# Strided attention on one core: another order of the first loads, TensorE's loop without its empty rounds, one tile for the blocks

## The chip, the core and the metric

The kernel runs on one core of a Trainium2 chip. The metric is the device time of one execution in microseconds, as a median over runs. The engines' names are those of the profile: PE is TensorE (PEld its weight loads), DVE VectorE, ACT ScalarE, POOL GpSimd, SP SyncE. SP computes nothing here; it issues every DMA, in the order of its program, and the sixteen DMA engines move the bytes. One DMA is one load or one store below.

## The reference

Every query attends to the 16 positions 0, 64, 128, ... of its own batch and head (8 x 12 heads, 1,024 positions, 64 values each).

```python
attend_positions = np.arange(0, seq, stride)
k = K[:, :, attend_positions, :].copy()
v = V[:, :, attend_positions, :].copy()
scores = np.einsum('bhqd,bhkd->bhqk', q, k) * scale
weights = np.exp(scores - np.max(scores, axis=-1, keepdims=True))
weights = weights / (np.sum(weights, axis=-1, keepdims=True) + 1e-10)
result[:, :, i, :] = np.einsum('bhqk,bhkd->bhqd', weights, v)[:, :, 0, :]
```

Q is 25.2 MB and so is the output, all float32. Of K and V only the 1,536 rows of 256 bytes at the attended positions are read, 384 KB each.

## The kernel before

The 96 heads are cut into 24 groups of four. A group's queries are one block of 1 MB, which lies in one of 18 buffers of 128 x 2,048 float32 (`qn`). A group's output is written into the buffer that held its queries, and stored from there. The buffers are nine tiles of two neighbours each (`pairs`), so that one store can send two groups, 2 MB. Loads are cut into 32 rows of 32 KB (`load`, issued through the helper at line 34).

For each group g the steps are:

- `cast`: the block is rounded to bfloat16 (`qb`) on POOL. For groups 0, 1 and 2 ACT takes one half (line 299) and POOL the other (line 301).
- `transpose` on DVE (line 316) into `qt`.
- `scores`: 16 matmuls on TensorE (line 324) with the prepared keys `k_t`.
- `largest` on DVE (lines 338 and 341), `raise_` on ACT (the exponential, line 346), `sums` on DVE (lines 351 and 354), `weights` on POOL (line 358).
- `turn`: four transposes of the weights on TensorE (line 365), then `spread` on ACT (line 377).
- `outputs`: eight matmuls (line 385) with the prepared values `v_all`, and `evict` on ACT (line 403), which brings the result from PSUM into the group's buffer.
- `queue`: the store on SP, and behind it late loads.

The keys are rounded once on ACT (line 263), transposed on DVE (line 264) and copied into `k_t` by DVE and ACT (line 273). The values are copied into `v_all` (line 287): the first eight small copies on POOL between its casts 0 and 1, the others later on ACT and POOL.

`Program` records every step with what it reads and writes and then gives each engine its instructions in the order in which they were recorded, with the semaphore waits between engines. `ORDER` (line 491) sets that order for the steady part. SP's order is: keys, Q block 0, values, Q blocks 1 to 17, and then what `queue` records. Since a late load takes the place of a stored group, it waits until that store has landed, and SP issues nothing else meanwhile.

TensorE's instructions are a loop of 13 turns of two rounds (`pe_stream`). Round i makes the scores of group i, the turn of group i - 2 and the outputs of group i - 3. Three counters, the gates `turned`, `weighted` and `free`, let a step begin. The last two rounds have no group of their own: their scores are made of old data and nobody reads them, and two memsets of one column of `edge` on DVE (line 314) open the gate for them. The outputs of group 23 stand behind the loop.

The last store, of group 23, is issued by itself at the end of the program, behind the wait of SP for the last eviction, while POOL waits for all older stores to land.

Of the kernel before, what the change touches and what calls it, by code (L numbers as in the profile page):

```python
# [10 lines left out]
FP32 = mybir.dt.float32  # L11
# [7 lines left out]
def _ap_with(ap: bass.AP, new_ap, extra_offset: int = 0) -> bass.AP:  # L19
    return dataclasses.replace(  # L20
        ap, ap=[list(p) for p in new_ap], offset=ap.offset + extra_offset
    )


def _copy(nc, out: bass.AP, in_: bass.AP):

    sides = [
        mybir.BassSymbolicTensorAccessPattern(
            ap=side.ap, dtype=side.dtype, bass_ap=side,
            is_dma=True, for_custom_bir_dma=True,  # L30
        )
        for side in (in_, out)
    ]
    return nc.sync.add_instruction(  # L34
        mybir.InstDMACopy(
            name=nc.get_next_instruction_name(), engine=mybir.EngineType.SP,
            ins=sides[:1], outs=sides[1:], queue="qSPDynamicHW",
            mode="Copy",
        )
    )  # L40


class Program:
# [13 lines left out]
    def op(self, engine, fn, reads=(), writes=(), after=(), lane=None, gate=None, gates=(), times=1, looped=False, last=False):  # L57
        i = len(self.ops)
        deps, own = set(after), set()
        for k in reads:  # L60
            deps.add(self.writer.get(k))
            own.add(self.writer.get(k))
        for k in writes:
            deps.update(self.readers.get(k, ()))
            deps.add(self.writer.get(k))
            own.add(self.writer.get(k))
        deps.discard(None)
        for k in reads:
            self.readers.setdefault(k, []).append(i)
        for k in writes:  # L70
            self.writer[k], self.readers[k] = i, []
        self.ops.append(dict(
            engine=engine, fn=fn, lane=lane or engine, deps=deps, own=own,
            gate=gate, gates=gates, times=times, last=last, looped=looped,
        ))
        return i
# [92 lines left out]
def kernel(  # L169
# [8 lines left out]
    nc = tc.nc  # L178

    B, H, S, D = Q.shape  # L180
# [3 lines left out]
    P = 128  # L184
    HG = 4
    NG = B * H // HG
    NC = NG // 2
    SD = S * D
    TURN = 2
    assert B * H == NG * HG and S == 1024 and D == 64 and NK == 16 and NG % TURN == 0  # L190
    BUFS = 18
    RUN = 2
    assert NG % RUN == 0 and BUFS % RUN == 0

    sb = ctx.enter_context(tc.tile_pool(name="sb", bufs=1))
    ps = ctx.enter_context(tc.tile_pool(name="ps", bufs=1, space=bass.MemoryType.PSUM))

    edge = sb.tile([P, 32], FP32, name="edge")
    pairs = [sb.tile([P, RUN, 32 * D], FP32, name=f"pair{i}") for i in range(BUFS // RUN)]
    qn = [pairs[i // RUN][:, i % RUN] for i in range(BUFS)]  # L200
    k_raw = sb.tile([P, NC, D], FP32, name="k_raw")
    k_bf, k_r = [sb.tile([P, NC, D], BF16, name=f"k_half{i}") for i in range(2)]
    v_raw = sb.tile([P, NC, D], FP32, name="v_raw")
# [20 lines left out]
    op = prog.op  # L224

    def load(g):
        n = 32
        op("SP", lambda: _copy(
            nc, qn[g % BUFS],
            _ap_with(Q, [[HG * SD // n, n], [1, HG * SD // n]], g * HG * SD),  # L230
        ), writes=[f"qn{g % BUFS}{h}" for h in range(2)], lane=f"q{g % BUFS}")
# [3 lines left out]
    def load_rows(name, tile_, src, lane):  # L235
        op("SP", lambda: nc.sync.dma_start(tile_, _ap_with(src, kv_src)),
           writes=[name], lane=lane)

    load_rows("k_raw", k_raw, K, "k")
    load(0)  # L240
    load_rows("v_raw", v_raw, V, "v")
    for g in range(1, BUFS):
        load(g)

    op("POOL", lambda: nc.gpsimd.memset(identity, 0.0), writes=["identity"])
# [1 line left out]
        out=identity, in_=identity, compare_op=ALU.not_equal, fill=1.0, base=0,  # L247
# [8 lines left out]
        out=sel, in_=identity.rearrange("p (q h k) -> p h q k", h=2, k=NK),  # L256
        op=ALU.max, axis=mybir.AxisListType.XY,
# [52 lines left out]
    def transpose(g):  # L310
        k_in = {0: "0", 1: "1"}.get(g)
        words = qt[g % 2].bitcast(I32)
        if g >= NG:
            op("DVE", lambda: nc.vector.memset(edge[:, g - NG : g - NG + 1], 0.0), gate="turned")
            return
        op("DVE", lambda: nc.vector.transpose(  # L316
            _ap_with(words, [words.ap[0], [1, 2], [D, 16], [2, 32]]), qb[g % 2].bitcast(I32),
        ), reads=[f"qb{g % 2}0", f"qb{g % 2}1"] + [f"k_t{k_in}{h}" for h in range(4) if k_in],
           writes=[f"qt{g % 2}"], gate="turned")
# [11 lines left out]
    def scores(g):  # L331
        op("PE", None, reads=[f"qt{g % 2}"] + [f"k_t{g % 2}{h}" for h in range(4)],
           writes=[f"sc{g % 2}"], gates=[("turned", g + 1)], looped=True)
# [23 lines left out]
    def weights(g):  # L357
        op("POOL", lambda: nc.gpsimd.tensor_tensor(  # L358
            out=wt[g % 2], in0=ex[g % 2],
            in1=rec[g % 2].unsqueeze(2).to_broadcast([P, 32, NK]), op=ALU.mult,  # L360
        ), reads=[f"ex{g % 2}", f"rec{g % 2}"] + [k for k in apart if k[0] == "v"], writes=[f"wt{g % 2}"], gate="weighted")

    def turn_products(g):
        for c in range(4):
            r = nc.tensor.transpose(  # L365
                tp_ps[g % 2][:, 2 * c : 2 * c + 2].rearrange("p a b -> p (a b)"),
                wt[g % 2][:, 8 * c : 8 * c + 8].rearrange("p t k -> p (t k)"), identity,
            )
        return r
# [12 lines left out]
    def output_products(g, k):  # L382
        for c in range(4):
            for u in range(2):
                r = nc.tensor.matmul(  # L385
                    _ap_with(
                        o_ps, [o_ps.ap[0], [128, 2], [256, 2], [1, D]],
                        extra_offset=512 * c + D * u,
                    ),
                    lhsT=wb[g % 2][:, 2 * c + u],  # L390
                    rhs=v_all[:, k].rearrange("p s d -> p (s d)"), start=True, stop=True,
                )
        return r
# [14 lines left out]
    def send(g, n):  # L408
        return _copy(
            nc,  # L410
            _ap_with(out, [[16 * D, P], [2 * SD, 2 * n], [1, 16 * D]], g * HG * SD),
            _ap_with(qn[g % BUFS], [pairs[0].ap[0], [1, 1], [1, 32 * n * D]]),
        )

    def store(g, n):
        op("SP", lambda: send(g, n), lane=f"out{g % BUFS // n}of{n}",
           reads=[f"qn{i % BUFS}{h}" for i in range(g, g + n) for h in range(2)])

    def idle(i):
# [29 lines left out]
    VALUES = {0: [(*q, "ACT") for q in large[:2]], 1: [(*q, "ACT") for q in large[2:4]]}  # L449
    VALUES.update((i + 2, [large[4 + i]]) for i in range(4))  # L450

    turns = (NG + 2) // TURN

    def queue(g):
        if g == NG - 2:
            store(g, 1)
        elif g % RUN == RUN - 1 and g < NG - 1:
            store(g - RUN + 1, RUN)
            late = BUFS + g - 2 * RUN + 1
            if BUFS <= late < NG:  # L460
                for n in range(late, late + RUN):
                    load(n)

    def at(i, stage, lag):
        g = i - lag
        if g in early.get(stage, ()):
            return
        if stage == "transpose" and 0 <= g < NG + 2:
            transpose(g)
        elif stage == "scores" and 0 <= g < NG + 2:  # L470
            scores(g)
        elif stage == "weights" and 0 <= g < NG:
            weights(g)
        elif stage == "turn" and 0 <= g < NG:
            turn(g)
        elif stage == "out" and -1 <= g < NG:
            outputs(g)
        elif stage == "spread" and 0 <= g < NG:
            spread(g)
        elif stage == "evict" and 0 <= g < NG:  # L480
            evict(g)
        elif stage == "cast" and 0 <= g < NG:
            cast(g, False)
        elif stage == "values" and g in VALUES:
            for q in VALUES[g]:
                values(*q)
        elif 0 <= g < NG and stage in stages:
            stages[stage](g)
# [3 lines left out]
    for i in range(1, NG + 5):  # L492
        for step in ORDER:
            name = step.rstrip("-0123456789")
            at(i, name, int(step[len(name):]))

    def pe_stream(sems, gates):
        pe = nc.tensor
        done = sems["PE"]
        pe.sem_inc(gates["weighted"], 2)  # L500
        pe.sem_inc(gates["free"], 3)
        with pe.Fori(0, turns) as turn_:
            for j in range(TURN):
                i = turn_ * TURN + j
                pe.wait_ge(gates["turned"], j + 1)
                score_products(j, i).then_inc(done, 1)
                pe.wait_ge(gates["weighted"], j + 1)
                turn_products(j).then_inc(done, 1)
                pe.wait_ge(gates["free"], j + 1)
                output_products(j + 1, i).then_inc(done, 1)  # L510
            for name in ("turned", "weighted", "free"):
                pe.sem_inc(gates[name], -TURN)

    pending, sems = prog.emit(pe_stream)
    with tc.tile_critical(sync_engine=mybir.EngineType.Pool, no_gpsimd_drain=True) as landed:
# [39 lines left out]
```

## Time and profile before

| | |
|---|---|
| median of 3 runs | 128.17 us (127.93 to 128.45) |
| the profiled execution, its own time | 127.63 us |
| its span, first to last instruction | 125.8 us |
| HBM read and written | 25.95 MB and 25.17 MB |
| mean rate over the span | 406 GB/s |
| loads of Q blocks | 24 of 1 MB |
| stores | 11 of 2 MB, 2 of 1 MB |
| granted clock of TensorE, mean | 0.867 |

How to read the lines of the profile that follow: a row of the timeline has start, duration, engine, line, operation and the tiles that it writes and reads (`pair<-in_Q_dram` is a load of a Q block, `out_dram<-pair` a store; buffer numbers are left out), a count, and in brackets the idle time before it with what ended it. SPq is SP's queue of instructions; its duration is that of the issue, not of the transfer. A row of DMA issues has a count, the size of one and the median time from issue to landing. A row of windows has the stretch, its length, busy time with the number of instructions of PE, PEld, DVE, ACT and POOL, the granted clock, the mean busy share of the DMA engines and GB/s; a packet's bytes are counted where the packet starts, so short stretches can show more or less than the true flow.

### The profile page before, as it was taken

The page shows a single profiled execution, that of the slowest core. Times are in us where ns is not written, and L with a number is a line of the kernel's source. Part 1 is how long each engine was busy: PE and PEld are TensorE (multiplying, and loading weights), DVE is VectorE, ACT ScalarE, POOL GpSimd, SP SyncE. Part 2 cuts the span into 40 slices and gives each one's busy share as a digit, 9 for nine tenths or more (in the row PEclk, how much of TensorE's full clock was granted, in tenths as well). Part 3 has the DMA queues.
Part 4 walks back from the last instruction along what each step waited for, and adds up shares of the span by engine and source line. Part 5 has one row for each costly group of instructions (what it writes and reads, how often), then busy time and mean ns, then how long its engine had stood idle before and what let it go on. Part 6 is the DMA issues. An engine that isn't in the chain of part 4 may idle for free.

```text
span 125.8 us, 2084 instructions
## 1 busy us (share of the span) xinstructions
PE 58.1 (46%) x736; PEld 43.5 (35%) x736; DVE 87.1 (69%) x131; ACT 93.8 (75%) x109; POOL 75.9 (60%) x67
## 2 busy tenths in 40 slices
PE   0007672556489466665555565666656533000000
PEld 0006452445366444443443344444434321000000
DVE  3795879999979899999999999999966100000000
ACT  4266756999888999999999999999999965000000
POOL 5648589999998688889888888879233300000000
PEclk9999999998555999999999999999999975555555
DMA  1998989989899998999999999999999999999991
GB/s 41 425 406 385 490 365 479 448 385 479 365 479 437 406 469 354 422 422 479 417 391 458 422 385 432 464 406 424 417 422 422 427 427 437 427 432 417 406 424 65
DMA packets 6132, 51.15 MB, mean 406 GB/s; under 512 B 3696, under 2 KB 3696, under 8 KB 3696
## 3 DMA queue, kind: packets, MB, share of 16 engines
q1 hardware_dynamic: 6128, 51.12, 96.8%
q14 instruction: 4, 0.03, 0.1%
HBM read 25.95 MB, written 25.17 MB: 406 GB/s over the span
## 4 chain that ended last, share of the span: by engine, by line
ACT 51%; POOL 15%; DVE 7%; DMA 5%; PE 4%; issue 1%; SPq 1%; POOLq 0%
ACT pair L403 28%; ACT wb_all L377 16%; ACT ex L346 7%; POOL qb L305 6%; DMA v_raw<-in_V_dram 5%; POOL wt_all L358 4%; PE o L385 4%; POOL v_all L287 4%; DVE qt L316 3%; DVE total L351 1%; DVE top L338 1%; DVE rec L354 1%; POOL qb L301 1%; SPq L34 1%; DVE low L341 1%
## 5 line engine op out<-in xcount | busy, mean ns | idle before, releaser
L403 ACT COPY pair<-o 128x2048 f32<-128x2048 f32 x24 | 47.9, 1995 | 2.8 <-PE o L385 2.8
L305 POOL CAST qb<-pair 128x2048 bf16<-128x2048 f32 x21 | 39.7, 1892 | 1.5 <-DMA pair<-in_Q_dram 1.5
L385 PE MATMUL o<-v_all,wb_all 128*128 (+1 forms) x216 | 31.6, 295 | 8.2 <-ACT pair L403 8.2
L358 POOL TENSOR_TENSOR wt_all<-ex,rec 128x512 bf16<-128x512 f32 x24 | 25.4, 1058 | 15.4 <-DVE rec L354 15.1
L377 ACT ACTIVATE wb_all<-tp,sel 128x512 bf16<-128x512 bf16 x48 | 33.3, 810 | 0.7 <-PE tp L365 0.6
L316 DVE STREAM_TRANSPOSE qt<-qb 128x1024 int32<-128x1024 int32 x24 | 29.8, 1242 | 1.2 <-POOL qb L305 0.7
L385 PEld LDWEIGHTS o<-v_all,wb_all 128*128 128x128 bf16 x216 | 20.7, 105 | 14.9 <-issue 9.6
L324 PE MATMUL sc<-k_t,qt 128*128 x416 | 19.4, 200 | 12.9 <-DVE qt L316 12.8
L324 PEld LDWEIGHTS sc<-k_t,qt 128*128 128x128 bf16 x416 | 16.9, 103 | 17.5 <-issue 16.6
L365 PE MATMUL tp<-identity,wt_all 128*128 128x128 bf16 x104 | 11.1, 235 | 25.5 <-POOL wt_all L358 25.5
L346 ACT ACTIVATE ex<-low 128x512 f32<-128x512 f32 x24 | 18.3, 764 | 2.5 <-DVE low L341 2.5
L351 DVE TENSOR_REDUCE total<-ex 128x32 f32<-128x512 f32 x24 | 16.3, 678 | 3.9 <-ACT ex L346 3.9
L341 DVE TENSOR_TENSOR low<-sc,top 128x512 f32<-128x512 f32 x24 | 16.6, 691 | 0.8
L365 PEld LDWEIGHTS tp<-identity,wt_all 128*128 128x128 bf16 x104 | 6.4, 103 | 28.3 <-POOL wt_all L358 28.2
L338 DVE TENSOR_REDUCE top<-sc 128x32 f32<-128x512 f32 x24 | 15.2, 632 | 1.3 <-PE sc L324 1.3
L354 DVE RECIPROCAL rec<-total 128x32 f32<-128x32 f32 x24 | 8.5, 353 | 0.8
L287 POOL CAST v_all<-v_raw 32x128 bf16<-32x128 f32 (+1 forms) x12 | 5.2, 431 | 1.5 <-DMA v_raw<-in_V_dram 0.8
L299 ACT CAST qb<-pair 128x1024 bf16<-128x1024 f32 x3 | 3.1, 1045 | 3.1 <-DMA pair<-in_Q_dram 3.1
L301 POOL CAST qb<-pair 128x1024 bf16<-128x1024 f32 x3 | 3.1, 1039 | 3.3 <-DMA pair<-in_Q_dram 3.3
L259 POOL MEMSET v_all<- 128x3456 f32 x1 | 3.0, 2979 | 0.0
L287 ACT CAST v_all<-v_raw 32x640 bf16<-32x640 f32 x4 | 2.9, 722 | 0.0
L250 DVE MEMSET k_t<- 128x1664 uint32 x1 | 1.4, 1445 | 1.9 <-issue 1.9
(15 smaller groups left out, 9.6 us busy)
## 6 DMA issues: line engine op xcount, KB each, us to landing
pair<-in_Q_dram SPq DMA_DIRECT2D x24, 1024.0 KB, 15.0
out_dram<-pair SPq DMA_DIRECT2D x11, 2048.0 KB, 22.8
out_dram<-pair SPq DMA_DIRECT2D x2, 1024.0 KB, 18.7
k_raw<-in_K_dram SPq DMA_DIRECT2D x1, 384.0 KB, 3.9
v_raw<-in_V_dram SPq DMA_DIRECT2D x1, 384.0 KB, 6.8
```

What stands on the lines that cost most here:

```text
L305: op("POOL", lambda: nc.gpsimd.tensor_copy(out=b, in_=q), reads=[f"qn{g % BUFS}{h}" for h in range(2)] + apart, writes=[f"qb{g % 2}{h}" fo ...
L316: op("DVE", lambda: nc.vector.transpose(_ap_with(words, [words.ap[0], [1, 2], [D, 16], [2, 32]]), qb[g % 2].bitcast(I32),), reads=[f"qb{g ...
L324: r = nc.tensor.matmul(sc_ps[g % 2][:, 64 * i : 64 * i + 64], lhsT=_ap_with(qt[g % 2], [qt[g % 2].ap[0], [2, P]], extra_offset=2 * P * i + f),
L338: op("DVE", lambda: nc.vector.tensor_reduce(out=m, in_=s, op=ALU.max, axis=mybir.AxisListType.X,), reads=[f"sc{g % 2}"], writes=[f"top{g % ...
L341: op("DVE", lambda: nc.vector.tensor_tensor(out=low, in0=s, in1=m.unsqueeze(2).to_broadcast([P, 32, NK]), op=ALU.subtract,), reads=[f"sc{g ...
L346: op("ACT", lambda: nc.scalar.activation(out=ex[g % 2], in_=low, func=AF.Exp, bias=0.0, scale=scale,), reads=["low"], writes=[f"ex{g % 2}"])
L351: op("DVE", lambda: nc.vector.tensor_reduce(out=total[g % 2], in_=ex[g % 2], op=ALU.add, axis=mybir.AxisListType.X,), reads=[f"ex{g % 2}"] ...
L358: op("POOL", lambda: nc.gpsimd.tensor_tensor(out=wt[g % 2], in0=ex[g % 2], in1=rec[g % 2].unsqueeze(2).to_broadcast([P, 32, NK]), op=ALU.mult,
L365: r = nc.tensor.transpose(tp_ps[g % 2][:, 2 * c : 2 * c + 2].rearrange("p a b -> p (a b)"), wt[g % 2][:, 8 * c : 8 * c + 8].rearrange("p t ...
L377: op("ACT", lambda a=a: nc.scalar.activation(out=wb[g % 2][:, :, 64 * a : 64 * a + 64], in_=tp_ps[g % 2], func=AF.Copy, scale=sel[:, a : a ...
L385: r = nc.tensor.matmul(_ap_with(o_ps, [o_ps.ap[0], [128, 2], [256, 2], [1, D]], extra_offset=512 * c + D * u,), lhsT=wb[g % 2][:, 2 * c + ...
L403: op("ACT", lambda: nc.scalar.copy(to, o_ps.rearrange("p c (b x) -> p c b x", b=2)), reads=["o"], writes=[f"qn{g % BUFS}{n}" for n in rang ...
```

## The change

It has three parts. The first loads go out as Q block 0, keys, Q block 1, values, Q blocks 2 to 17. TensorE's loop has 12 turns, so it covers the 24 groups alone; the turns of groups 22 and 23 and the outputs of groups 21 and 22 follow it as straight code, and the two rounds of empty scores and their memsets are gone. The 18 buffers are one tile, `q_all`; the runs of groups that one store sends are written as a table (11 of two groups, then group 22 alone), and the late loads are taken from a list.

```diff
-    RUN = 2
+    RUNS = {**{g: 2 for g in range(0, NG - 2, 2)}, NG - 2: 1}
+    ENDS = {g + n - 1: (g, n) for g, n in RUNS.items()}
...
-    pairs = [sb.tile([P, RUN, 32 * D], FP32, name=f"pair{i}") for i in range(BUFS // RUN)]
-    qn = [pairs[i // RUN][:, i % RUN] for i in range(BUFS)]
+    q_all = sb.tile([P, BUFS, 32 * D], FP32, name="q_all")
+    qn = [q_all[:, i] for i in range(BUFS)]
...
+    load(0)
     load_rows("k_raw", k_raw, K, "k")
-    load(0)
+    load(1)
     load_rows("v_raw", v_raw, V, "v")
-    for g in range(1, BUFS):
+    for g in range(2, BUFS):
         load(g)
...
-        if g >= NG:
-            op("DVE", lambda: nc.vector.memset(edge[:, g - NG : g - NG + 1], 0.0), gate="turned")
-            return
...
-        op("SP", lambda: send(g, n), lane=f"out{g % BUFS // n}of{n}",
+        op("SP", lambda: send(g, n), lane=f"out{g % BUFS}",
...
-    turns = (NG + 2) // TURN
+    turns = NG // TURN
+
+    late = list(range(BUFS, NG))
 
     def queue(g):
-        if g == NG - 2:
-            store(g, 1)
-        elif g % RUN == RUN - 1 and g < NG - 1:
-            store(g - RUN + 1, RUN)
-            late = BUFS + g - 2 * RUN + 1
-            if BUFS <= late < NG:
-                for n in range(late, late + RUN):
-                    load(n)
+        if g not in ENDS:
+            return
+        first, n = ENDS[g]
+        store(first, n)
+        while late and late[0] - BUFS < first:
+            load(late.pop(0))
...
+        for j in range(2):
+            pe.wait_ge(gates["weighted"], j + 1)
+            turn_products(j).then_inc(done, 1)
+            pe.wait_ge(gates["free"], j + 1)
+            output_products(j + 1, NG + j).then_inc(done, 1)
```

More of the change, by code (lines that the diff above doesn't have):

```diff
@@ L191 @@
     BUFS = 18
-    RUN = 2
-    assert NG % RUN == 0 and BUFS % RUN == 0
+    RUNS = {**{g: 2 for g in range(0, NG - 2, 2)}, NG - 2: 1}
+    ENDS = {g + n - 1: (g, n) for g, n in RUNS.items()}
     sb = ctx.enter_context(tc.tile_pool(name="sb", bufs=1))
@@ L411, in send @@
             _ap_with(out, [[16 * D, P], [2 * SD, 2 * n], [1, 16 * D]], g * HG * SD),
-            _ap_with(qn[g % BUFS], [pairs[0].ap[0], [1, 1], [1, 32 * n * D]]),
+            _ap_with(qn[g % BUFS], [q_all.ap[0], [1, 1], [1, 32 * n * D]]),
         )
     def store(g, n):
-        op("SP", lambda: send(g, n), lane=f"out{g % BUFS // n}of{n}",
+        op("SP", lambda: send(g, n), lane=f"out{g % BUFS}",
            reads=[f"qn{i % BUFS}{h}" for i in range(g, g + n) for h in range(2)])
@@ L467, in at @@
             return
-        if stage == "transpose" and 0 <= g < NG + 2:
+        if stage == "transpose" and 0 <= g < NG:
             transpose(g)
-        elif stage == "scores" and 0 <= g < NG + 2:
+        elif stage == "scores" and 0 <= g < NG:
             scores(g)
```

## The prediction

> **What bounds the kernel now.** I read the page's slices and DMA parts first, because the table of engines shows none above 75%.
>
> ```profile
> span 125.8 us, 2084 instructions
> PE 58.1 (46%) x736; PEld 43.5 (35%) x736; DVE 87.1 (69%) x131; ACT 93.8 (75%) x109; POOL 75.9 (60%) x67
> DMA  1998989989899998999999999999999999999991
> q1 hardware_dynamic: 6128, 51.12, 96.8%
> ACT 51%; POOL 15%; DVE 7%; DMA 5%; PE 4%; issue 1%; SPq 1%; POOLq 0%
> ```
>
> The sixteen DMA engines are busy in every slice but the first and the last, for 96.8% of the span, all on the one queue that SP feeds. The chain that ended last names ACT, but it is followed back from the last engine instruction, so what happens after that instruction isn't in it. The timeline of the end shows the difference, and the issues from 106 us on show how long the last store took.
>
> ```profile
> 102.88 0.54 SPq L34 DMA_DIRECT2D out_dram<-pair  x1
> 104.83 1.87 ACT L403 COPY pair<-o 128x2048 f32<-128x2048 f32 x1 [1.98 <-PE o L385]
> 107.28 0.54 SPq L34 DMA_DIRECT2D out_dram<-pair  x1
> out_dram<-pair SPq DMA_DIRECT2D x1, 1024.0 KB, 19.7
> out_dram<-pair SPq DMA_DIRECT2D x1, 1024.0 KB, 17.8
> ```
>
> The last eviction ends at 106.70. The last store is issued at 107.28 and lands 17.8 later, at 125.1; the one before it goes out at 102.88 and lands 19.7 later, at 122.6. All arithmetic is over 18 us before the end, and those 18 us are stores that wait for their turn.
>
> That transfers wait in line all along shows in the rates by stretch (last column GB/s) and in the times to landing.
>
> ```profile
> 15.00:40.00 25.00, 15.97 (x202) 12.61 (x197) 22.56 (x34) 21.11 (x27) 23.14 (x19) 0.82 1.02 438
> 40.00:70.00 30.00, 18.21 (x247) 13.56 (x245) 29.01 (x43) 30.00 (x36) 25.07 (x18) 0.98 0.99 422
> 70.00:100.00 30.00, 17.25 (x244) 12.82 (x241) 25.19 (x42) 30.00 (x35) 18.71 (x14) 1.00 1.00 424
> 100.00:122.00 22.00, 2.83 (x16) 1.61 (x15) 0.00 (x0) 4.67 (x4) 0.00 (x0) 0.56 1.00 425
> out_dram<-pair SPq DMA_DIRECT2D x11, 2048.0 KB, 22.8
> ```
>
> The rate is 422 to 438 whatever the engines do. A 2 MB store moves in 2.097 MB / 424 = 4.9 us, yet it lands 22.8 us after its issue: some 18 us of other transfers lie ahead of it. So the span is one line of transfers, and its end is start of the line + what the line loses before it runs at full rate + bytes / rate. Only the first two can change here.
>
> **The start of the line.** These are SP's first issues and the first work that each load releases, then the rates in the first microseconds.
>
> ```profile
> 0.96 0.43 SPq L236 DMA_DIRECT2D k_raw<-in_K_dram  x1
> 1.45 0.74 SPq L34 DMA_DIRECT2D pair<-in_Q_dram  x1
> 3.10 12.33 SPq L34 DMA_DIRECT2D pair<-in_Q_dram  x17
> 4.86 0.83 ACT L263 CAST k_half<-k_raw 128x768 bf16<-128x768 f32 x1 [2.26 <-DMA k_raw<-in_K_dram]
> 7.29 1.04 ACT L299 CAST qb<-pair 128x1024 bf16<-128x1024 f32 x1 [1.60 <-DMA pair<-in_Q_dram]
> 9.13 2.75 POOL L287 CAST v_all<-v_raw 32x128 bf16<-32x128 f32 x8 [0.77 <-DMA v_raw<-in_V_dram]
> 11.47 1.04 ACT L299 CAST qb<-pair 128x1024 bf16<-128x1024 f32 x1 [1.04 <-DMA pair<-in_Q_dram]
> 13.87 1.05 ACT L299 CAST qb<-pair 128x1024 bf16<-128x1024 f32 x1 [0.50 <-DMA pair<-in_Q_dram]
> 1.50:2.00 0.50, 0.00 (x0) 0.00 (x0) 0.10 (x1) 0.50 (x1) 0.26 (x2) 1.00 0.07 16
> 2.00:3.00 1.00, 0.00 (x0) 0.00 (x0) 1.00 (x1) 0.60 (x1) 1.00 (x2) 1.00 0.39 86
> 3.00:4.00 1.00, 0.00 (x0) 0.00 (x0) 0.83 (x2) 0.00 (x0) 1.00 (x1) 1.00 1.21 261
> ```
>
> The releases are 4.86 (keys), 7.29 (Q block 0), 9.13 (values), 11.47 (Q block 1), 13.87 (Q block 2). So inside the line a Q block costs 2.34 to 2.43 us (I use 2.40), and the values, of the same size and shape as the keys, cost 9.13 - 7.29 = 1.84. The keys, first in the line, cost 4.86 - 0.96 = 3.90 from their issue: 2.06 more than the values. The rates say where a part of this lies: from 2 to 3 us only 86 GB/s flow, then 261, which is the rate of these 256-byte rows. What moved in that microsecond would take 86 / 261 = 0.33, so **0.67 us is lost in a slow first microsecond**. The other 2.06 - 0.67 = 1.39 is issue, first byte and landing, which any first transfer pays.
>
> **The change, part by part.**
>
> *Order of the first loads.* The same four transfers, with Q block 0 moved ahead of the keys and Q block 1 ahead of the values, on the same queue; two DMA issues pass two others on SP, nothing is added. The sum of the four inside the line is unchanged (2 x 2.40 + 2 x 1.84 = 8.48). What changes is who pays the slow first microsecond. No row shows a Q block at the head of an empty line, so I bound it. If the slowness belongs to the keys (1,536 small rows, and few of them under way at first), a Q block of large rows skips it and the keys' own slow beginning passes while Q block 0 moves for 2.4 us: gain 0.67. If it belongs to the first microsecond of any transfer, the gain is 0. The issue of a Q block is also longer than that of the keys, 0.74 against 0.43 in the rows above: loss up to 0.31. But that 0.74 was taken behind another issue. Later, behind a wait, two of them took 1.11 (row below), so one takes some 0.55, and I take 0.10. Of the ramp's two bounds I take 0.67, because what is short in that microsecond looks like rows: 86 GB/s are 336 rows of 256 bytes in 1 us, and 261 are 1,020, while the code cuts a whole Q block into 32 pieces. A limit on rows that lets 336 through doesn't touch 32. **Gain 0.67 - 0.10 = 0.57; bounds -0.31 and +0.67.**
>
> ```profile
> 60.72 1.11 SPq L34 DMA_DIRECT2D pair<-in_Q_dram  x2
> ```
>
> *What is late because of it.* With the gain, Q block 0 lands at 0.96 + 1.49 + 2.40 = 4.85, the keys at 6.69, Q block 1 at 9.09, the values at 10.93. On ACT the rounding of the keys waits in front of its half of cast 0, so cast 0 now follows the keys; on DVE the key copies and transpose 0 follow them. The keys are 1.83 later and the values 1.80, so all arithmetic starts about 1.8 us later. Its cover: the last eviction then ends at 108.5 and the last store enters the line near 109.1, while the line is full up to the landing of the store before it, then 122.6 - 0.57 = 122.0. That leaves over 12 us. The first store is the other place: it is issued at 29.60, and the last of the first 18 loads, whose issue of some 0.6 ends at 3.10 + 12.33 = 15.43, lands at 14.8 + 35.5 = 50.3, so 1.8 us later still finds 18 us of line. Cost 0; without that cover it would be 1.8.
>
> ```profile
> 29.60 8.83 SPq L34 DMA_DIRECT2D out_dram<-pair  x2
> pair<-in_Q_dram SPq DMA_DIRECT2D x1, 1024.0 KB, 35.5
> 55.39 1.30 SPq L34 DMA_DIRECT2D pair<-in_Q_dram  x2
> SPq L34 <- DMA out_dram<-pair: 28.2, 3, 17.0
> ```
>
> *Late loads.* Load 18 waits on SP for the first store to land, at 55.39, and everything behind it on SP waits too. Before, the store of groups g-1 and g is followed by loads g+15 and g+16 (18 and 19 behind groups 2 and 3). After, it is followed by the loads n with n - 18 below g-1: again 18 and 19 there, then 20, 21 and 22, 23. Same order, same three waits: 0.
>
> *TensorE's loop.* Two rounds of score products are dropped, 32 matmuls, and with them two memsets on DVE of 59 ns. The last two rounds of turns and outputs come as 24 matmuls behind the loop, with the same waits.
>
> ```profile
> 97.34 0.63 PE L324 MATMUL sc<-k_t,qt 128*128 x16
> 99.15 0.40 PE L365 MATMUL tp<-identity,wt_all 128*128 128x128 bf16 x4 [1.18 <-POOL wt_all L358]
> L314 DVE MEMSET edge<- 128x1 f32 x2 | 0.1, 59 | 0.0
> ```
>
> Each dropped round is 0.63 us, and TensorE then sits idle for 1.18 until POOL has the weights: nothing. Leaving the loop could cost a fetch of code that no row shows; the nearest bound is the 1.18 that it idles here anyway, and beyond that the 12 us of line cover it.
>
> *One tile.* The 18 buffers were nine tiles of two. Sizes, rows and counts of all transfers stay: 0, unless something waits for the whole tile (second rival).
>
> **The sum.** Against the profiled run's own 127.63 (span 125.8 and 1.83 around it): 127.63 - 0.57 = 127.06. The runs' median, 128.17, lies 0.54 above that run, so I forecast **127.6**.
>
> **The rivals.**
>
> 1. *The slow first microsecond belongs to the start of the line.* Then Q block 0 pays it, and the issue's 0.10 to 0.31 comes on top: 128.3 to 128.5, no change that can be told. For it: 16 GB/s before 2 us and 86 after it could be DMA engines that start one by one. Against: the share of busy DMA time in that row, 0.39, stands over all sixteen engines at work on short rows as well as over six of them. The Trainium skill ("DMA: Bandwidth & Descriptors", Anatomy of one DMA, given there for the path through GpSimd) speaks for this rival: a transfer's fixed cost, about 2.0 us, scales with nothing. By that rule the ramp's gain would be 0; the 2.06 of the keys agrees in size, though no run here shows that path.
>
> 2. *Slower: the last store waits for the older ones.* It is placed behind all else and now reads the same tile as every store. If it came to wait for their landing, it would be issued at 122.0, into an empty line, and pay 2.06 + 2.40 there: it would land at 126.5 instead of 125.1, so the time would be 128.17 + 1.4 = 129.6. It decides as soon as that wait exists. Against: the last group's buffer (slot 5) already shared a tile with two older stores (slot 4, used twice), and its issue at 107.3 waited for neither.
>
> 3. *The arithmetic sets the end.* The delay of 1.8 would have to grow beyond the 12 us of line left, by a stall of TensorE behind its loop, say; each microsecond beyond costs one. With 2 beyond, it would be 127.6 + 2 = 129.6. Against: nothing near 14 us of stall shows anywhere in TensorE's rows above, which have 1.18.
>
> **How the numbers follow.** The forecast gets 0.62, rival 1 0.26, rival 2 0.08, rival 3 0.04. A measurement can tell 0.5%, 0.64 us, from no change. The forecast's gain of 0.57 lies just inside that, with runs from 127.93 to 128.45 around it, and the full ramp of 0.67 just outside, so I split it about in half: 0.33 faster, 0.29 within. Of rival 1, 0.21 is within, and its upper end, a quarter of a per cent above the median before, puts with the runs' scatter 0.05 on the slow side, to which rivals 2 and 3 add 0.12. Faster 0.33, within 0.50, slower 0.17. The range runs from the full 0.67 of gain on a low run (128.17 - 0.67 - 0.5 = 127.0) up to rival 1's upper end, 128.5; rivals 2 and 3 are left out.
>
> **What would show it.** Right: SP's first issue is Q block 0 at about 0.96, Q block 0 lands near 4.9 and the keys near 6.7, the values' copies on POOL start near 10.9, and every landing behind them is 0.5 to 0.6 earlier, the last near 124.5; the rate between 2 and 3 us is several times 86. Rival 1: that rate is low again and the values' copies start at 11.5 or later. Rival 2: the last issue comes after 120. Rival 3: a slice before the last one shows idle DMA engines. The loop and the tile are misjudged if the late loads' issues (55.39, 60.72) move by more than the start of the line did.

## The result and the profile after

| | before | after |
|---|---|---|
| median of 20 runs, us | 128.12 | 128.68 |
| lowest and highest | 127.86, 128.72 | 128.11, 129.43 |
| ratio, 95% interval | | 1.0048 [1.0036, 1.006] |
| span, median of the runs | 126.2 (35 runs, in the first experiment) | 126.6 (20 runs) |
| the profiled execution, its own time and span | 127.63, 125.8 | 128.52, 126.7 |

The kernel became slower by 0.56 us, where 0.57 us of gain had been forecast. These are the lines of the changed kernel's page that answer to those of before; the buffers are now called `q_all`, and line numbers have moved by a few.

```profile
span 126.7 us, 2005 instructions
DMA  6699999899898998999999999999999999999991
q1 hardware_dynamic: 6128, 51.12, 96.8%
q8 instruction: 1, 0.02, 0.0%
ACT 50%; POOL 16%; PE 9%; DMA 5%; issue 3%; DVE 3%; SPq 0%; POOLq 0%; DVEq 0%
```

The DMA engines are as busy as before, so the kernel still ends with its line of transfers. Two things differ. The first slice is fuller (6 instead of 1), and yet the whole is longer: a piece under way counts as busy time also when it is slow. And there is a transfer that the page of before doesn't have: one packet of instructions, 0.02 MB, on a queue of its own.

The start of the line, from the timeline and from the windows (the last column is GB/s, with a packet's bytes booked where it starts):

```profile
0.96 0.58 SPq L34 DMA_DIRECT2D q_all<-in_Q_dram  x1
1.60 0.56 SPq L236 DMA_DIRECT2D k_raw<-in_K_dram  x1
2.20 1.47 SPq L34 DMA_DIRECT2D q_all<-in_Q_dram  x1
3.71 0.59 SPq L236 DMA_DIRECT2D v_raw<-in_V_dram  x1
6.30 1.04 POOL L302 CAST qb<-q_all 128x1024 bf16<-128x1024 f32 x1 [1.28 <-DMA q_all<-in_Q_dram]
7.71 0.83 ACT L264 CAST k_half<-k_raw 128x768 bf16<-128x768 f32 x1 [5.11 <-DMA k_raw<-in_K_dram]
11.61 2.38 POOL L288 CAST v_all<-v_raw 32x128 bf16<-32x128 f32 x7 [4.27 <-DMA v_raw<-in_V_dram]
2.00:3.00 1.00, 0.00 (x0) 0.00 (x0) 1.00 (x1) 0.60 (x1) 1.00 (x2) 1.00 1.89 500
3.00:4.00 1.00, 0.00 (x0) 0.00 (x0) 0.83 (x2) 0.00 (x0) 1.00 (x1) 1.00 0.08 33
4.00:5.00 1.00, 0.00 (x0) 0.00 (x0) 0.95 (x2) 0.00 (x0) 1.00 (x1) 1.00 1.29 524
```

Block 0 is there at 6.30, not at 4.85; the keys at 7.71, not at 6.69; the values' copies start at 11.61, not at 10.93. The windows show what block 0 does: 500 GB/s begin between 2 and 3 us (a piece of 32 KB on nearly every DMA engine, booked where it starts), almost nothing begins between 3 and 4, and the second 16 pieces come between 4 and 5. So the first pieces take nearly 2 us. In the trace they last 1.94 us on average, where a piece in the steady line lasts 1.21. The prediction's sign for being right, a rate between 2 and 3 us of several times 86, came true and misled: the 500 are bytes that only began to move. The landings decide, and the values' start at 11.61 is rival 1's sign.

The end, from the timeline, and from the issues in 110 to 113 us:

```profile
108.19 1.86 ACT L401 COPY q_all<-o 128x2048 f32<-128x2048 f32 x1 [1.98 <-PE o L383]
110.63 0.54 SPq L34 DMA_DIRECT2D out_dram<-q_all  x1
out_dram<-q_all SPq DMA_DIRECT2D x1, 1024.0 KB, 15.3
```

The last eviction ends at 110.05, 3.35 us later than before, and the last store still stands 15.3 us in line, landing at 125.9. The delay of the arithmetic is larger than the 1.8 forecast, but it is hidden, as the prediction had it. The order alone (e1 below) delayed the last eviction by 1.83, so something else adds to it. The granted clock (PEclk, the sixth entry) is one part of it, here first before and then after:

```profile
98.00:100.00 2.00, 0.49 (x5) 0.33 (x6) 0.00 (x0) 2.00 (x3) 1.06 (x1) 1.00 0.99 418
99.90 1.04 PE L385 MATMUL o<-v_all,wb_all 128*128 x8 [0.35 <-ACT pair L403]
98.00:100.00 2.00, 1.94 (x11) 1.28 (x12) 0.89 (x2) 2.00 (x4) 0.00 (x0) 0.50 1.01 426
102.42 1.89 PE L383 MATMUL o<-v_all,wb_all 128*128 128x256 bf16 x8 [0.46 <-ACT q_all L401]
```

Without the empty rounds the steps behind the loop ran at a granted clock of 0.50, and the outputs of group 22 took 1.89 us instead of 1.04. In all five traces without these rounds the clock had fallen to 0.50 for good by 100 us; in nine of the ten that keep them (e11 left aside, with its late start), this came at 102 to 109 us, in e14 at 96. The prediction had put the loss of the empty rounds at nothing; for the time that holds, because of the line. e4, which keeps them, was 3.03 later too, so they are not the whole of it.

### The profile page after: what moved, and what is told of

Same layout as the page of the kernel before. It is cut to its first block, busy times and chain, and to the rows that moved or that the text cites. A ratio compares the mean times of both kernels' runs of the same rounds, so it can differ in the third digit from the quotient of the medians.

```text
span 126.7 us, 2005 instructions
## 1 busy us (share of the span) xinstructions
PE 59.0 (47%) x704; PEld 43.2 (34%) x704; DVE 86.3 (68%) x129; ACT 93.6 (74%) x109; POOL 75.8 (60%) x67
## 4 chain that ended last, share of the span: by engine, by line
ACT 50%; POOL 16%; PE 9%; DMA 5%; issue 3%; DVE 3%; SPq 0%; POOLq 0%; DVEq 0%
ACT q_all L401 28%; ACT wb_all L375 15%; POOL qb L306 8%; PE o L383 7%; ACT ex L344 7%; POOL wt_all L356 5%; DMA k_raw<-in_K_dram 5%; POOL v_all L288 2%; DVE k_t L274 1%; DVE qt L314 1%; PE sc L322 1%; PE tp L363 1%; POOL qb L302 1%; ACT k_half L264 1%; DVE k_half L265 0%
## 5 line engine op out<-in xcount | busy, mean ns | idle before, releaser
L401 ACT COPY q_all<-o 128x2048 f32<-128x2048 f32 x24 | 47.9, 1995 | 3.9 <-PE o L383 3.9
L306 POOL CAST qb<-q_all 128x2048 bf16<-128x2048 f32 x21 | 39.7, 1890 | 0.1
L383 PE MATMUL o<-v_all,wb_all 128*128 (+1 forms) x216 | 33.3, 306 | 8.3 <-ACT q_all L401 8.3
L383 PEld LDWEIGHTS o<-v_all,wb_all 128*128 128x128 bf16 x216 | 21.4, 108 | 16.1 <-issue 8.9
L322 PE MATMUL sc<-k_t,qt 128*128 x384 | 18.0, 201 | 15.4 <-DVE qt L314 15.2
L322 PEld LDWEIGHTS sc<-k_t,qt 128*128 128x128 bf16 x384 | 15.7, 103 | 19.7 <-issue 18.8
L264 ACT CAST k_half<-k_raw 128x768 bf16<-128x768 f32 x1 | 0.8, 831 | 5.1 <-DMA k_raw<-in_K_dram 5.1
L302 POOL CAST qb<-q_all 128x1024 bf16<-128x1024 f32 x3 | 3.1, 1037 | 1.4 <-DMA q_all<-in_Q_dram 1.3
L300 ACT CAST qb<-q_all 128x1024 bf16<-128x1024 f32 x3 | 3.1, 1037 | 0.0
L265 DVE STREAM_TRANSPOSE k_half<-k_half 128x384 int32<-128x384 int32 x1 | 0.6, 578 | 3.5 <-ACT k_half L264 3.5
```

The source lines that it names most:

```text
L306: op("POOL", lambda: nc.gpsimd.tensor_copy(out=b, in_=q), reads=[f"qn{g % BUFS}{h}" for h in range(2)] + apart, writes=[f"qb{g % 2}{h}" fo ...
L322: r = nc.tensor.matmul(sc_ps[g % 2][:, 64 * i : 64 * i + 64], lhsT=_ap_with(qt[g % 2], [qt[g % 2].ap[0], [2, P]], extra_offset=2 * P * i + f),
L383: r = nc.tensor.matmul(_ap_with(o_ps, [o_ps.ap[0], [128, 2], [256, 2], [1, D]], extra_offset=512 * c + D * u,), lhsT=wb[g % 2][:, 2 * c + ...
L401: op("ACT", lambda: nc.scalar.copy(to, o_ps.rearrange("p c (b x) -> p c b x", b=2)), reads=["o"], writes=[f"qn{g % BUFS}{n}" for n in rang ...
```

## The experiments

Every kernel ran beside the kernel before on the same chip; medians are compared with that one's, 127.92 to 128.09.

**First set: one part at a time.** `e1_order` has the new order alone:

```diff
-    load_rows("k_raw", k_raw, K, "k")
     load(0)
+    load_rows("k_raw", k_raw, K, "k")
+    load(1)
     load_rows("v_raw", v_raw, V, "v")
-    for g in range(1, BUFS):
+    for g in range(2, BUFS):
```

> The kernel before with the new order of the first loads alone. Three theories. (F) The code behind TensorE's loop has to be fetched: a transfer of 16 KB of instructions at 106.35 us in the changed kernel's profile, 1.0 us on one of the sixteen DMA engines, and a store is there only when its slowest engine is. By F the order is worth what the start shows, the values landing 0.04 later than block 1 did: ratio 0.999 to 1.001, no 16 KB fetch. (O) The order costs the 0.56 us: ratio 1.003 to 1.006 here. (T) The single tile costs it: ratio 1.000 here. The last eviction should end 2 us later in each case, hidden.

`e2_loop` has the loop of 12 turns with the straight code behind it, `e3_tile` the one tile with the table of runs, and `e4_no_loop` is the changed kernel with the old loop.

> The kernel before with the loop of 12 turns and its last steps behind it alone. F: a 16 KB instruction transfer near 103 us, the landings of the stores behind it 0.3 to 0.6 later, ratio 1.002 to 1.005. O and T: ratio 1.000, and the landings as before.

> The kernel before with the one tile and the table of runs alone. F and O: ratio 1.000, same landings. T: 1.003 to 1.006.

> The changed kernel with the old loop of 13 turns (order and tile stay). F: no 16 KB transfer, ratio 0.999 to 1.001. O or T: 1.003 to 1.006.

| | median, us | ratio, interval | span, median | runs with over 2.4 us outside the span |
|---|---|---|---|---|
| before | 127.93 | | 126.2 | 0 of 35 |
| e1_order | 128.29 | 1.0009 [0.9982, 1.0036] | 126.5 | 0 of 12 |
| e2_loop | 128.17 | 1.0012 [0.9984, 1.004] | 125.9 | 6 of 12 |
| e3_tile | 127.86 | 0.999 [0.9966, 1.0014] | 126.1 | 0 of 12 |
| e4_no_loop | 128.31 | 1.0018 [0.9995, 1.0042] | 126.5 | 0 of 12 |

None of these ratios is clear of 1 by itself. But two things stand out. The two kernels with the new order have spans that are 0.3 longer by the median. And the loop does nothing to the span: it acts on the time outside it, that is the run's time less its span. That is 1.72 to 1.83 us in every run of the kernel before, and 2.43 to 2.84 in half of e2's runs. In the changed kernel it is 2.61 to 2.88 in 7 of 20 runs. My expectation F, that the instructions' transfer delays the stores, missed this: it looked inside the line. It may not be wholly wrong there: the changed kernel's 7 runs have spans of 126.4 by the median, its 13 others 126.7, so that the 7 are 0.64 longer by their mean times and not a whole microsecond. In e2 the two halves differ by 0.1 in span. The tile costs nothing.

**Second set: which move, and whose code.** `e5_block0_first` moves block 0 ahead of the keys and leaves the values in front of block 1. `e6_values_late` moves the values alone.

```diff
 e5: load(0); keys; values; load(1) ...
 e6: keys; load(0); load(1); values; load(2) ...
```

> The kernel before with Q block 0 ahead of the keys alone (order: block 0, keys, values, block 1). Two theories of the order's cost (e1_order: 0.36 us by the medians, span 0.3 longer). (H) What stands at the head of the empty line pays the cold start, and a Q block pays more than the keys: its first pieces took 1.7 to 1.9 us instead of 1.2 and began 0.25 later. Then this kernel costs as much as e1_order: median 0.3 to 0.4 over the kernel before, block 2 landing at 14.1 to 14.4. (V) The cost comes from the values behind block 1: then this one costs 0 to 0.1, block 2 at 13.8.

> The kernel before with the values behind Q block 1 alone (order: keys, block 0, block 1, values). H: 0 to 0.1 over the kernel before, block 2 landing at 13.8. V: 0.3 to 0.4 over it, block 2 at 14.1 or later.

`e7_code_behind` adds instructions behind the old loop that do nothing, and `e8_code_ahead` adds some ahead of the new one:

```diff
 e7, behind the loop of 13 turns:
+        for _ in range(52):
+            pe.wait_ge(done, 1)
 e8, ahead of the loop of 12 turns:
+        for _ in range(96):
+            pe.wait_ge(gates["free"], 1)
```

> The kernel before with 52 waits on TensorE behind its loop that are all met already: as many instructions as the straight code of the change adds, and no other change. In e2_loop the span did not grow, but in half of its runs the time outside the span was 2.4 to 2.8 us instead of 1.8. (C) That comes of the length of TensorE's code, whose end lies in a part that is not there yet: then this kernel shows the same, 2.4 to 2.9 outside the span in a third to two thirds of its runs, span as before, median 0.1 to 0.5 higher. (W) It comes of the work in the straight steps or of the loop's end: then this kernel has 1.7 to 1.85 outside in every run, ratio 1.000.

> e2_loop with 96 waits on TensorE ahead of its loop, all met already: the straight code behind the loop lies 96 instructions further on. C: where the code lies decides; a fetch for it falls elsewhere, so the share of runs with 2.4 to 2.9 us outside the span changes clearly, to none or to all. W: the share stays near a half.

| | median, us (before: 127.95) | ratio, interval | span, median (before: 126.2) | over 2.4 us outside |
|---|---|---|---|---|
| e5_block0_first | 129.09 (5 runs; a sixth took 131.55) | 1.0111 [1.0073, 1.015] | 127.3 | 0 of 6 |
| e6_values_late | 128.05 | 1.0005 [0.9994, 1.0015] | 126.3 | 0 of 12 |
| e7_code_behind | 128.01 | 1.0002 [0.9989, 1.0016] | 126.2 | 0 of 12 |
| e8_code_ahead | 127.86 | 1.0 [0.9985, 1.0015] | 126.1 | 0 of 12 |

e6 shows that the values behind block 1 are free, which leaves block 0 ahead of the keys as what costs (H). But e5 costs three times what was expected: with the keys and values next to each other a second loss appears. SP's timeline of e5:

```profile
0.96 0.58 SPq L34 DMA_DIRECT2D pair<-in_Q_dram  x1
1.60 0.56 SPq L236 DMA_DIRECT2D k_raw<-in_K_dram  x1
2.20 0.89 SPq L236 DMA_DIRECT2D v_raw<-in_V_dram  x1
3.13 14.30 SPq L34 DMA_DIRECT2D pair<-in_Q_dram  x17
```

The first of the 17 issues, of block 1, takes 3.9 us in the trace, and the block lands 3.11 us behind the values instead of some 2.40. The held issue is not the loss by itself: in e1 the first issue behind the values took 3.67, and its block landed 2.38 behind them. Nor is e5 later than e1 because of block 1, since its keys came sooner: block 2 lands at 14.43 (e1: 14.40) and block 16 at 48.55 (48.51). The two part at block 17, the last of the first loads: it lands 3.11 behind block 16 in e5, and 2.42 to 2.44 behind it in every kernel whose row loads go out on SP with a block between them. What delays it is not known. The change, with block 1 between the row loads, doesn't have this loss.

e8 supports C: the same straight code, 48 instructions further on (two waits come as one), and no run has the extra microsecond. e7 seemed to speak against C, but its 52 waits were 26 instructions, half of what the straight code adds.

**Third set.** `e9_code_behind_52` repeats e7 with 108 waits, 54 instructions. `e12_after_code_ahead` is the changed kernel with e8's 96 waits ahead of its loop.

> e7_code_behind with 108 waits behind TensorE's loop instead of 52: in e7's profile two waits came as one instruction, so that it added 26 instructions where the change's straight code adds about 50; here it is 54. C (the end of TensorE's code, or what follows it, isn't there when it is reached): 2.4 to 2.9 us outside the span in a third to two thirds of the runs, the span as before. W (the work of the straight steps does it): 1.7 to 1.85 outside in all runs.

> The changed kernel with 96 waits on TensorE ahead of its loop, as in e8_code_ahead. C: no run has more than 1.85 us outside the span, the span stays that of the changed kernel (126.4 to 126.7), so the median is about 0.35 over the kernel before (ratio 1.002 to 1.004): the order alone is left. W: a third or more of the runs keep 2.4 to 2.9 outside, ratio 1.004 to 1.006.

`e10_small_first` puts a load of 16 KB in front of the changed kernel's block 0, and `e11_keys_from_act` lets ACT issue the keys of the kernel before, so that they and block 0 move at once.

```diff
 e10, ahead of load(0):
+    op("SP", lambda: nc.sync.dma_start(edge, _ap_with(Q, [[S, P], [1, 32]])), writes=["edge"], lane="first")
 e11, in place of the keys' load on SP:
+    op("ACT", lambda: nc.scalar.dma_start(k_raw, _ap_with(K, kv_src)), writes=["k_raw"], lane="k")
```

> The changed kernel with a load of 128 rows of 128 bytes into the unused tile `edge` ahead of Q block 0. H1 (the first microsecond of an empty line is slow for whatever moves in it): the small load takes it, block 0's first pieces take some 1.3 us, and in spite of one more issue of 0.45 us block 2 lands at 13.7 to 14.0, span 0.2 to 0.4 under that of the changed kernel (126.6 by its median). H2 (a Q block is slow at first because of its own large pieces): block 0's pieces take 1.7 to 1.9 again, block 2 lands at 14.3 or later, span as the changed kernel or longer.

> The kernel before with the keys' load issued by ACT, so that Q block 0 is first on SP and both move at once. H1: the slow first microsecond is paid once by both together; the 0.4 us or so in which few of the keys' rows flow carry pieces of block 0 too, block 2 at 13.4 to 13.8, ratio 0.996 to 1.000. H2: block 2 at 13.9 or later, ratio 1.000 to 1.003.

| | median, us (before: 127.92) | ratio, interval | span, median (before: 126.1) | over 2.4 us outside |
|---|---|---|---|---|
| e9_code_behind_52 | 128.65 | 1.005 [1.003, 1.007] | 126.4 | 5 of 10 |
| e10_small_first | 129.48 | 1.0105 [1.007, 1.014] | 127.0 | 3 of 6 |
| e11_keys_from_act | 159.01 | 1.2424 [1.2388, 1.246] | 157.3 | 0 of 6 |
| e12_after_code_ahead | 128.38 | 1.0045 [1.003, 1.006] | 126.6 | 0 of 10 |

C holds. 54 idle instructions behind the old loop, and nothing else, bring the extra microsecond in half of the runs. The DMA part of e9's profile for the window 120 to 131 us, which goes beyond the span's end at 126.3 (a slice is 0.275 us):

```profile
DMA  9999999799976322000000000000020000000000
q1 hardware_dynamic: 222, 1.55, 33.5%
q8 instruction: 1, 0.02, 0.7%
```

The line of stores runs out, nothing moves for some 3 us, and then, near 128.0, behind the last profiled instruction, one 16 KB packet of instructions is fetched. This run took 129.02, 2.8 more than its span. e10's trace (below) has the packet at 128.9, and 2.7 outside. In the changed kernel's own profile the same packet lies in the window 100 to 107, inside the line, and that run had 1.8 outside:

```profile
q1 hardware_dynamic: 201, 3.01, 101.4%
q8 instruction: 1, 0.02, 0.9%
```

So the packet is read in the line in some runs and at the very end in others. In e8 and e12 it was inside the line too, at 98.6 and 100.6, and none of their 22 runs had the extra time. One trace fits neither case: e2's has no such packet, neither in the line nor up to 131 us, and 1.95 outside. Why the cases fall about half and half is open. With the fetch inside the line, e12 shows what the order costs in a kernel that has all else of the change: 0.46 us by the medians, a little more than the 0.35 expected.

e10 refutes H1 in the form that a small load could take the slow beginning upon itself: block 0's first pieces lasted 1.87 us again, and the small load came on top.

e11 is a miss by 31 us, and its profile shows why. The keys' row by tile, the DMA row of the page, and a window:

```profile
L263 ACT CAST k_half<-k_raw x1: 832/832/832, 50.5 to 50.5; 128x768 bf16<-128x768 f32 x1
DMA  5999999999995000000938999999989999997994
q10 hardware_dynamic: 1552, 0.39, 1.1%
55.00:70.00 15.00, 11.83 (x131) 9.45 (x132) 12.98 (x19) 10.51 (x15) 10.69 (x9) 1.00 0.00 0
```

The keys have a queue of their own (q10), and they land at 50.5, with the last of the 18 blocks: after each piece of 32 KB only one or two rows of 256 bytes get their turn on a DMA engine, every 1.2 us. Arithmetic starts 46 us late, and the line is empty from 55 to 70. The Trainium skill says ("DMA: Bandwidth & Descriptors", Queues, rings and completion order) that a DMA engine takes turns between the queues packet by packet; this trace shows what that does where one queue's packets are 128 times as long. The Trainium skill gives 9 to 17 descriptors as typical of one turn; here it was one or two rows.

**Fourth set: why block 0 is slow at the head.** `e13_blocks_first` loads blocks 0, 1 and 2 ahead of keys and values; `e14_block0_finer` is e1 with block 0 in 128 pieces of 8 KB (`n = 32 if g else P`).

> The kernel before with Q blocks 0, 1 and 2 ahead of the keys and the values. A Q block at the head of the line had its first 16 pieces of 32 KB in 1.7 to 1.9 us each, where later ones take 1.21. (G) That comes of the rows' descriptors: in all kernels with block 0 first the keys, 1,536 rows, were issued right behind it and prepared while it moved. Here nothing but blocks is prepared then: first pieces 1.2 to 1.3, block 2 landing at about 0.96 + 1.4 + 3 x 2.43 = 9.7. (L) Large pieces are slow in an empty line whatever stands behind: first pieces 1.6 to 1.9 again, block 2 landing at 10.3 to 10.7. The keys come some 6 us later than before, which the line's 12 us still cover; span 126.0 to 126.3 by G, 126.4 to 126.8 by L.

> e1_order with block 0 cut into 128 rows of 8 KB instead of 32 of 32 KB. L in the form that the size of the pieces matters: the head costs less, block 0 lands under 5.9 (e1: 6.22) and the span is 0.2 or more shorter than that of e1_order. G, or L in the form that only the start of the line matters: block 0 lands at 6.1 to 6.4, the span as that of e1_order (126.5).

| | median, us (before: 128.09) | ratio, interval | span, median (before: 126.3) |
|---|---|---|---|
| e13_blocks_first | 129.50 | 1.0117 [1.0099, 1.0135] | 127.7 |
| e14_block0_finer | 128.32 | 1.0017 [1.0005, 1.0028] | 126.5 |

From e13's timeline and its windows:

```profile
0.95 2.17 SPq L34 DMA_DIRECT2D pair<-in_Q_dram  x3
3.17 0.60 SPq L236 DMA_DIRECT2D k_raw<-in_K_dram  x1
3.81 4.64 SPq L236 DMA_DIRECT2D v_raw<-in_V_dram  x1
2.00:3.00 1.00, 0.00 (x0) 0.00 (x0) 1.00 (x1) 0.59 (x1) 1.00 (x2) 1.00 1.51 401
3.00:4.00 1.00, 0.00 (x0) 0.00 (x0) 0.83 (x2) 0.00 (x0) 1.00 (x1) 1.00 0.32 131
4.00:5.00 1.00, 0.00 (x0) 0.00 (x0) 0.96 (x2) 0.00 (x0) 1.00 (x1) 1.00 1.32 524
```

The keys are issued at 3.17 only, and still hardly anything begins between 3 and 4: the first pieces lasted 1.81 us and block 0 landed at 6.20. So the keys' descriptors are not to blame (G falls). e13 also has keys and values side by side: the values' issue takes 4.64 us, the block behind them lands 3.13 later instead of 2.43, and block 17 lands 3.42 behind block 16. Up to block 16 the line is nearly level with e1's (48.68 and 48.51), so most of what makes its span miss even L comes at block 17. Block 2 landed at 11.16, also later than L had it.

In e14 small pieces are slow as well, as its windows show:

```profile
2.00:3.00 1.00, 0.00 (x0) 0.00 (x0) 1.00 (x1) 0.60 (x1) 1.00 (x2) 1.00 0.16 41
3.00:4.00 1.00, 0.00 (x0) 0.00 (x0) 0.82 (x2) 0.00 (x0) 1.00 (x1) 1.00 0.90 360
```

Block 0 landed at 6.34, and only 41 GB/s begin in the first microsecond. So neither the size of the pieces nor what stands behind them matters. The packets in the traces say a little more. In each of e1, e4, e5 and e12 eight of the first sixteen pieces began before 2.8 us and lasted 1.7 to 2.3 us; the other eight began at 2.9 to 3.3 and lasted 1.2 to 1.5. So about 3 us on, pieces move almost as in the steady line. It is not the first bytes in the line that decide: in e10 a small load went first, block 0 was issued 0.45 later, and twelve pieces that began at 2.7 to 3.1 still lasted 1.7 to 2.3. What makes this stretch slow is not settled.

## Why the prediction was wrong

**What bounds the kernel, the cover, the late loads, the tile.** Right. The line of transfers sets the end, the arithmetic was 3.35 us later without showing, the first two late loads were issued behind the same stores at 55.43 and 61.12 (55.39 and 60.72 before), and e3 found nothing in the tile. No run showed a last store that waits (rival 2): its issue came at 110.63.

**The step that failed: "Of the ramp's two bounds I take 0.67, because what is short in that microsecond looks like rows."** Block 0 was to skip the slow start and land 1.49 over its 2.40. It landed at 6.12 to 6.25 in the profiles of e1, e4, e5, e12, e13 and of the changed kernel, which is 5.2 us after its issue, 2.8 over its 2.40. So the gain of 0.67 was not there, and rival 1 was right in this.

The price with which both were worked out, the 2.06 that the keys pay at the head, was too low as well. It came from one profile, and the kernels with the keys first left six more. These are the keys, block 0 and the values of e8:

```profile
5.65 0.83 ACT L263 CAST k_half<-k_raw 128x768 bf16<-128x768 f32 x1 [3.05 <-DMA k_raw<-in_K_dram]
8.10 1.04 ACT L299 CAST qb<-pair 128x1024 bf16<-128x1024 f32 x1 [1.62 <-DMA pair<-in_Q_dram]
9.54 2.74 POOL L287 CAST v_all<-v_raw 32x128 bf16<-32x128 f32 x8 [0.38 <-DMA v_raw<-in_V_dram]
```

By the landings the keys took 3.87 us from their issue in the profile before, and 4.11 to 4.66 in e2, e3, e6, e7, e8 and e9. The values took 1.73 behind a block there (the 1.84 was read at POOL's start), and 1.34 to 1.36 in the six. So the keys pay 2.1 over the values in the first profile and 2.8 to 3.3 in the others, about as much as block 0 pays. Either load pays at the head.

What made a loss of it is the other half of the same step, that "the keys' own slow beginning passes while Q block 0 moves". Behind block 0 the keys took 1.42 to 2.01 us, where values take 1.34; in e13, behind block 2, the keys took 1.33. So behind block 0 they took 0.1 to 0.7 more than inside the line. The term "gain 0.57" measures as a loss of 0.36 (e1) to 0.46 (e12) by the medians. These pieces don't add up to it closely, since single profiles scatter by 0.5 us: block 2 lands at 13.88 to 14.40 in e1, e4, e12 and the changed kernel, and at 13.72 to 14.29 in the seven with the keys first. The medians of the spans carry the size: 126.5 or 126.6 for these four, against 125.9 to 126.4 for the seven. The bytes of the packets carry the place: the four had moved 15 MB 0.35 us later than the seven by the mean, and 51 MB 0.38 later, so nearly all is lost in the first 40 us.

**The step on TensorE's loop: "Leaving the loop could cost a fetch of code that no row shows ... the 12 us of line cover it."** The fetch was named and its place was wrong. Half the time it comes when the line is over, where nothing covers it. The sum took the 1.83 us around the span as fixed, and that is where time went: 1 us in 7 of 20 runs, about 0.34 on average, or 0.22 when the shorter spans of these 7 runs are counted in. The Trainium skill ("Runtime: NRT & Kernel Launch", Instruction fetch mechanics) says that code is refilled in blocks of 16 KiB and that the cost of crossing into a new one is mostly hidden. The packet has that size here; in e8 and e12 no run has the extra time outside the span, and in half of the runs of e9 it is there. The loop alone costs 0.24 by the medians (e2), the order with the tile 0.38 (e4), and together they make up the 0.56 within what these medians can tell. Rival 1's upper end, 128.5, left this fetch out.

No version of these beats the kernel before; e8, with the shorter loop and its code moved, equals it.

## What to carry to other kernels

Where the DMA line is full from start to end, putting another load at its head need not gain anything: here small rows and a large block paid about the same there, and the rows paid a part again behind the block. Take the price of such a start from several profiles, since one was 0.6 to 1.2 us below the six others. Keep two loads of small rows apart: the two kernels that had them side by side lost another 0.7 us and more. A few dozen more instructions on an engine can move a code fetch behind the last instruction, where the span doesn't show it, so compare the time outside the span as well. Don't put small rows on a second queue beside large pieces if anything early waits for them.

## What the runs showed of the hardware

- A block of 1 MB at the head of an empty line lands 5.2 us after its issue; in the full line one lands every 2.43 us. A load of 1,536 rows of 256 bytes lands 3.9 to 4.7 us after its issue at the head, and mostly takes 1.34 in the line.
- With two loads of 1,536 rows each issued one behind the other, the block behind them landed 3.11 (e5) and 3.13 us (e13) after them instead of some 2.4, and block 17 landed 3.11 and 3.42 after block 16 instead of 2.43.
- A fetch of 16 KB of instructions at 128.0 us, 1.7 us behind the end of the span, goes with 0.6 to 1.2 us more outside the span.
- Rows of 256 bytes beside pieces of 32 KB on another queue took 49 us to land, against 3.9 to 4.7 at the head of SP's own queue.
- Without the matmuls whose results nobody reads, the granted clock of TensorE fell to 0.50 by 98 us in the changed kernel (102.5 before), and eight matmuls of the outputs took 1.89 us instead of 1.04.
